# A decoder trunk on one core: other homes in SBUF for the operands of TensorE

## The chip, the core and the metric

The kernel runs on 1 core of one Trainium2 chip. The metric is the time of one execution in microseconds, as the device reports it; lower is better. A core has TensorE (PE; its weight loads are listed apart as PEld), VectorE (DVE), ScalarE (ACT), GpSimd (POOL) and SyncE (SP), which issues most of the DMAs. SBUF, the memory that the engines read their operands from, has 128 partitions; a tile has one home, a range of bytes, which is the same in each partition it spans.

## What is computed

Two layers of a decoder trunk on 256 tokens of width 1024, in float32. Each layer is a half-step SwiGLU with LayerNorm, three token mixers in parallel on one normalised stream, an output projection with LayerNorm, and a second half-step SwiGLU with LayerNorm.

```python
def hybrid_layer(x, mem_n, ...):
    h = layer_norm(ALPHA * x + 0.5 * swiglu(x, ffn1_w_gu, ffn1_w_down), ln_g[0], ln_b[0])
    (dn_q, dn_k, dn_v, dn_b, dn_a, dn_z, sw_q, sw_k, sw_v, xa_q, gates) = jnp.split(h @ w_in, split_idx, axis=-1)
    o_dn = deltanet_branch(...)            # gated delta rule, 4 heads of 128
    o_sw = sliding_window_attention(...)   # 8 query heads of 64, window 128, sinks
    o_xa = memory_cross_attention(...)     # 4 heads of 128 over 256 memory rows
    branches = jnp.stack([o_dn, o_sw, o_xa], axis=2)
    gates = sigmoid(gates.reshape(B, S, 3, D))
    merged = sum(gates * einsum('bsnc,ncd->bsnd', branches, w_branch), axis=2)
    h = layer_norm(ALPHA * h + merged @ w_out, ln_g[1], ln_b[1])
    return layer_norm(ALPHA * h + 0.5 * swiglu(h, ffn2_w_gu, ffn2_w_down), ln_g[2], ln_b[2])
```

`swiglu(x, w_gu, w_down)` is `(silu(gate) * up) @ w_down` with 2816 columns for each of gate and up.

## The kernel before

All weights come as one long stream from DRAM (`wst`), in units of 128 partitions x 1024 columns (512 KB), in the order of their use. `unit` (from line 99) loads a unit with a DMA on SP's queue into one of three buffers `raw` and splits it in two: ScalarE rounds it into `whi`, VectorE puts the remainder into `wlo` (`split`, line 116 in the profile's lists, five buffers of each). A product of full precision is then three matmuls in a fast format (`mm3`): high by high, high by low, low by high. The matmuls are recorded by one helper on line 125, those of the first block of an FFN also on lines 318, 319 and 321. The order of the instructions on an engine is that of a scheduler, with some stretches held in the order of the program.

A matmul has a stationary operand, which a weight load brings into TensorE, and a moving one, which is streamed past it. The names in the profile stand as `out<-moving,stationary`. Every matmul here is preceded by its own weight load. The kinds that matter:

- The transposed stream `hT` (eight blocks of 128 channels, high and low halves, 16 KB a partition) is stationary in the FFNs' first projections and in the gates; the split weights move, 512 columns at a time (`acc<-whi,hT`, `acc<-wlo,hT`). In the combined input projection of the mixers 324 columns move, and where an output is wanted transposed (`projB`) the split weights are stationary and 256 columns of `hT` move (`acc<-hT,whi`).
- The FFN's inner columns after the SwiGLU stand in `u0` to `u10`, each 4 KB a partition: 2 of the 22 column blocks, with high and low halves. They are stationary in the second projection (`acc<-whi,u`), block by block from `u0` on, 12 matmuls of 512 columns for most blocks. The mixers use `u0` to `u13` and `w0` to `w3` again for their own tiles, among them the branches' outputs, the memory's transposed rows and the merged stream (`w0` to `w3`).
- The last units of a second projection or of the output projection are split ahead of time into `u` and `w` tiles that are free by then and in `gt` and `pp`; there the names read `acc<-u,u` or `acc<-u,w`.

Tiles get their homes by pool, in the order in which the pools are opened, and within a pool by a tag's first use:

```python
pc = ctx.enter_context(tc.tile_pool(name="pc", bufs=1))
praw = ctx.enter_context(tc.tile_pool(name="praw", bufs=3))
phi = ctx.enter_context(tc.tile_pool(name="phi", bufs=5))
plo = ctx.enter_context(tc.tile_pool(name="plo", bufs=5))
pu = ctx.enter_context(tc.tile_pool(name="pu", bufs=1))
p2 = ctx.enter_context(tc.tile_pool(name="p2", bufs=2))
...
def T(pool, shape, tag, dt=F32, bufs=None):
    kw = {} if bufs is None else {"bufs": bufs}
    return pool.tile(shape, dt, tag=tag, name=nm(tag), **kw)
```

`pc` holds constants, masks, the residual stream `h0` and `h1` and the window attention's keys `swk`; `pu` holds `hT`, the `u` and `w` tiles and all that exists once; `p2` and `p3` hold what is used in turns (`t2`, `pt`, `pp`, `gt`). A slice of `hT`, of a `u` or `w` tile or of a split weight, as a matmul takes it, always starts at a multiple of 512 bytes from the tile's start, save for the 324 columns mentioned.

Of the kernel before, what the change touches and what calls it, by code (L numbers as in the profile page):

```python
# [37 lines left out]
@with_exitstack  # L38
def tile_trunk(ctx, tc, x, xT, mem, memT_, wst, lnp, memln, cvw, rows, cst, out):
    nc = tc.nc  # L40
    pc = ctx.enter_context(tc.tile_pool(name="pc", bufs=1))
    praw = ctx.enter_context(tc.tile_pool(name="praw", bufs=3))
    phi = ctx.enter_context(tc.tile_pool(name="phi", bufs=5))
    plo = ctx.enter_context(tc.tile_pool(name="plo", bufs=5))
    pu = ctx.enter_context(tc.tile_pool(name="pu", bufs=1))
# [8 lines left out]
    def nm(s):  # L54
        uid[0] += 1
        return f"{s}_{uid[0]}"

    def T(pool, shape, tag, dt=F32, bufs=None):
        kw = {} if bufs is None else {"bufs": bufs}
        return pool.tile(shape, dt, tag=tag, name=nm(tag), **kw)  # L60

    def acc():
        return T(psA, [P, 512], "acc")

    def at():
        return T(psT, [P, 512], "at")

    def sm():
        return T(psS, [P, 512], "sm")
# [161 lines left out]
    def new_hT():  # L231

        t = T(pu, [P, KD, 2, S], "hT", F32R)
        return t[:, :, 0, :], t[:, :, 1, :], t
# [791 lines left out]
    hT = new_hT()  # L1026
# [20 lines left out]
    for l in range(NL):  # L1047
# [18 lines left out]
        if not last:  # L1066
            f1, hT = Ffn(), post.hT
# [88 lines left out]
```

## Time and profile before

| | |
|---|---|
| time, median of 3 runs (lowest to highest) | 1295.89 us (1292.63 to 1296.61) |
| the profiled execution: its time, its span | 1294.92 us, 1293.1 us |
| granted TensorE clock, mean over the span | 0.995 |
| busy: PE, PEld, DVE, ACT, POOL | 1269.7, 1076.4, 855.6, 662.0, 201.2 us |
| DMA | 263.50 MB, mean 204 GB/s |

The span reaches from the first to the last instruction of the program. The duration of a matmul runs from its start to its end, and since matmuls are pipelined, the next one starts before that; the spacing of the starts is worked out from the first and last start of a group and its count. Rows of groups show count, busy time, mean duration and the idle time of the engine before them with what ended it; rows of a single tile show duration as min/median/max, and first and last start.

### The profile page before, as it was taken

The page shows a single profiled execution, that of the slowest core. Times are in us where ns is not written, and L with a number is a line of the kernel's source. Part 1 is how long each engine was busy: PE and PEld are TensorE (multiplying, and loading weights), DVE is VectorE, ACT ScalarE, POOL GpSimd, SP SyncE. Part 2 cuts the span into 40 slices and gives each one's busy share as a digit, 9 for nine tenths or more (in the row PEclk, how much of TensorE's full clock was granted, in tenths as well). Part 3 has the DMA queues.
Part 4 walks back from the last instruction along what each step waited for, and adds up shares of the span by engine and source line. Part 5 has one row for each costly group of instructions (what it writes and reads, how often), then busy time and mean ns, then how long its engine had stood idle before and what let it go on. Part 6 is the DMA issues. An engine that isn't in the chain of part 4 may idle for free.

```text
span 1293.1 us, 18743 instructions
## 1 busy us (share of the span) xinstructions
PE 1269.7 (98%) x6944; PEld 1076.4 (83%) x6944; DVE 855.6 (66%) x1273; ACT 662.0 (51%) x979; POOL 201.2 (16%) x361
## 2 busy tenths in 40 slices
PE   8999899999999999999999999999999999999997
PEld 6887688999878788888888888899988787888886
DVE  5676557698555776665676665758866378766555
ACT  5555443566574545454445444446556655455441
POOL 1232100102411002221012220000023100022200
PEclk9999899999999999999999999999999999999999
DMA  7887763654543648877768776656554256487762
GB/s 265 300 286 250 245 235 124 215 174 131 148 159 125 202 134 268 257 243 219 256 202 263 246 237 214 205 165 205 169 142 155 98 174 234 140 265 242 238 217 102
DMA packets 78075, 263.50 MB, mean 204 GB/s; under 512 B 11968, under 2 KB 13120, under 8 KB 77984
## 3 DMA queue, kind: packets, MB, share of 16 engines
q1 hardware_dynamic: 66320, 232.53, 54.8%
q0 software_dynamic: 11664, 29.77, 7.9%
q8 instruction: 54, 0.88, 0.3%
q14 instruction: 37, 0.30, 0.1%
HBM read 247.45 MB, written 14.81 MB: 203 GB/s over the span
## 4 chain that ended last, share of the span: by engine, by line
PE 83%; DMA 7%; DVE 4%; ACT 3%; issue 2%; POOL 0%; SPq 0%; DVEq 0%; ACTq 0%; POOLq 0%
PE acc L125 72%; DMA raw<-in_wst_dram 6%; PE at L125 4%; PE sm L125 3%; DVE wlo L116 2%; ACT whi L116 2%; PE sm L128 1%; PE acc L321 1%; PE acc L318 1%; PE acc L319 1%; PE at L128 1%; DVE u L116 0%; DMA gB<-ms 0%; DMA tr<-t 0%; ACT pp L724 0%
## 5 line engine op out<-in xcount | busy, mean ns | idle before, releaser
L116 DVE TENSOR_TENSOR wlo<-raw,whi 128x1024 fp32r<-128x1024 f32 (+2 forms) x403 | 484.8, 1209 | 331.9 <-ACT whi L116 329.5
L116 ACT CAST whi<-raw 128x1024 fp32r<-128x1024 f32 (+2 forms) x403 | 415.3, 1036 | 442.2 <-PE acc L125 209.8
L125 PE MATMUL acc<-whi,hT 128*128 128x512 f32 (+1 forms) x1824 | 563.6, 387 | 5.0 <-ACT whi L116 5.0
L125 PEld LDWEIGHTS acc<-whi,hT 128*128 128x128 f32 x1824 | 341.1, 188 | 73.1 <-ACT whi L116 5.0
L125 PE MATMUL acc<-wlo,hT 128*128 128x512 f32 (+1 forms) x912 | 351.1, 385 | 0.8 <-DVE wlo L116 0.8
L125 PE MATMUL acc<-whi,u 128*128 128x512 f32 x784 | 256.1, 400 | 5.9 <-DVE t L340 5.9
L125 PEld LDWEIGHTS acc<-wlo,hT 128*128 128x128 f32 x912 | 171.9, 188 | 34.5 <-DVE wlo L116 2.3
L125 PEld LDWEIGHTS acc<-whi,u 128*128 128x128 f32 x784 | 149.2, 190 | 42.2 <-DVE t L340 4.8
L125 PE MATMUL acc<-wlo,u 128*128 128x512 f32 x392 | 155.8, 398 | 0.0
L349 POOL DMA_DIRECT2D tr<-t x176 | 96.6, 556 | 354.6 <-DVE t L343 339.4
L125 PE MATMUL acc<-hT,whi 128*128 128x256 f32 x672 | 122.2, 284 | 0.0
L125 PEld LDWEIGHTS acc<-hT,whi 128*128 128x128 f32 x672 | 104.7, 192 | 0.0
L125 PE MATMUL acc<-hT,wlo 128*128 128x256 f32 x336 | 95.0, 283 | 0.0
L125 PEld LDWEIGHTS acc<-wlo,u 128*128 128x128 f32 x392 | 74.7, 191 | 16.5
L125 PEld LDWEIGHTS acc<-hT,wlo 128*128 128x128 f32 x336 | 64.4, 192 | 0.0
L350 POOL DMA_DIRECT2D pt<-tr x44 | 25.1, 571 | 183.5 <-DMA tr<-t 132.7
L339 ACT ACTIVATE t<-acc 128x256 f32<-128x256 f32 x88 | 32.9, 379 | 22.7 <-PE acc L125 22.7
L340 DVE TENSOR_TENSOR t<-t,acc 128x256 f32<-128x256 f32 x88 | 36.3, 417 | 6.5 <-ACT t L339 3.6
L116 DVE TENSOR_TENSOR u<-pt,u 128x512 fp32r<-128x512 f32 x44 | 29.0, 659 | 12.1 <-ACT u L116 12.1
L524 DVE SCALAR_TENSOR_TENSOR t<-acc,cw,t 128x255 f32<-128x255 f32 (+2 forms) x72 | 34.5, 479 | 0.9
L116 ACT CAST u<-pt 128x512 fp32r<-128x512 f32 x44 | 27.0, 613 | 14.4 <-DMA pt<-tr 14.4
L125 PE MATMUL acc<-whi,w 128*128 128x512 f32 x96 | 31.7, 401 | 2.1 <-DVE w L116 2.1
(248 smaller groups left out, 1188.5 us busy)
## 6 DMA issues: line engine op xcount, KB each, us to landing
raw<-in_wst_dram SPq DMA_DIRECT2D x409, 512.0 KB, 4.3
tr<-t POOLq DMA_DIRECT2D x176, 64.0 KB, 3.6
pt<-tr POOLq DMA_DIRECT2D x44, 256.0 KB, 4.7
raw<-in_wst_dram SPq DMA_DIRECT2D x16, 324.0 KB, 2.9
gB<-in_lnp_dram SPq DMA_DIRECT2D x6, 512.0 KB, 6.1
bB<-in_lnp_dram SPq DMA_DIRECT2D x6, 512.0 KB, 5.6
mdr<-w POOLq DMA_DIRECT2D x4, 512.0 KB, 7.2
w<-dr POOLq DMA_DIRECT2D x4, 512.0 KB, 10.6
```

The source lines that it names most:

```text
L116: return nc.scalar.copy(hi, src).ins, nc.vector.tensor_tensor(lo, src, hi.bitcast(F32), op=ALU.subtract).ins
L125: return pe(nc.tensor.matmul(*a, **k))
L128: return pe(nc.tensor.transpose(*a))
L318: nc.tensor.matmul(ps, hT[0][:, k, ts], hi[:, c], start=k == 0, stop=False)
L319: nc.tensor.matmul(ps, hT[0][:, k, ts], lo[:, c], start=False, stop=False)
L321: nc.tensor.matmul(ps, hT[1][:, k, ts], hi[:, c], start=False, stop=k == KD - 1)
L339: act = nc.scalar.activation(t[:, :, tb, :], g, AF.Silu).ins
L340: ins = nc.vector.tensor_tensor(t[:, :, tb, :], t[:, :, tb, :], u, op=ALU.mult).ins
L349: nc.gpsimd.dma_start(d[:, :, q].rearrange("b c x -> c b x"), z[32 * q:32 * q + 32].rearrange("c (b x) -> c b x", b=4))
L350: nc.gpsimd.dma_start(y, d.rearrange("b c q x -> (b c) (q x)"))
L524: nc.vector.scalar_tensor_tensor(yc[:, j, d:], b[:, j, :S - d], w[:, t:t + 1], yc[:, j, d:], op0=ALU.mult, op1=ALU.add)
```

## The change

A new pool `pn` is opened ahead of all others, and the tiles with the tags `hT`, `u0` to `u13` and `w0` to `w3`, which were in `pu`, are put there. All else keeps its pool, and pools behind it move up.

```diff
+    pn = ctx.enter_context(tc.tile_pool(name="pn", bufs=1))
     pc = ctx.enter_context(tc.tile_pool(name="pc", bufs=1))
     praw = ctx.enter_context(tc.tile_pool(name="praw", bufs=3))
     phi = ctx.enter_context(tc.tile_pool(name="phi", bufs=5))
...
+    NEAR = {"hT"} | {f"u{i}" for i in range(14)} | {f"w{i}" for i in range(4)}
+
     def T(pool, shape, tag, dt=F32, bufs=None):
+        pool = pn if pool is pu and tag in NEAR else pool
         kw = {} if bufs is None else {"bufs": bufs}
         return pool.tile(shape, dt, tag=tag, name=nm(tag), **kw)
```

The two built programs have the same instructions on each engine in the same order, with the same shapes and the same waits; the homes alone differ. Bytes within a partition, from the first to behind the last, and in brackets the first byte modulo 128:

| tiles | before | after |
|---|---|---|
| `hT` | 87584 to 103968 (32) | 16512 to 32896 (0) |
| `u0`, `u1`, `u2` | 103968 to 116256 (32) | 32896 to 45184 (0) |
| two small tiles, 320 bytes | 116256 to 116576 | 177696 to 178016 |
| `w0` to `w3` | 116576 to 132960 (96) | 45184 to 61568 (0) |
| `u3` to `u13`, with `gB` and `bB` among them before | 132960 to 186208 (96) | 61568 to 106624 (0), `gB` and `bB` at 178016 |
| constants, `swk` (`swk` at 32), `h0`, `h1` | 16512 to 34336 | 106624 to 124448 |
| `raw`, 3 buffers | 34336 to 46624 (32) | 124448 to 136736 (32) |
| `whi`, 5 buffers | 46624 to 67104 (32) | 136736 to 157216 (32) |
| `wlo`, 5 buffers | 67104 to 87584 (32) | 157216 to 177696 (32) |
| `sql` (the window attention's low queries) | 187840 to 191936 (64) | the same |
| `t2`, `pt`, `pp`, `gt` | 192992 to 225760 (96) | the same |

## The prediction

> **What bounds the kernel now.** I read the page first (engines, slices, the chain that ended last), then the waits of TensorE, then the groups kept apart by shape, then single tiles in short stretches.
>
> ```profile
> PE 1269.7 (98%) x6944; PEld 1076.4 (83%) x6944; DVE 855.6 (66%) x1273; ACT 662.0 (51%) x979; POOL 201.2 (16%) x361
> PEclk9999899999999999999999999999999999999999
> PE 83%; DMA 7%; DVE 4%; ACT 3%; issue 2%; POOL 0%; SPq 0%; DVEq 0%; ACTq 0%; POOLq 0%
> ...
> PE acc L125 <- DVE t L340: 5.9, 4, 3.4
> PE acc L125 <- ACT whi L116: 5.0, 1, 5.0
> PE acc L125 <- DVE w L116: 2.1, 2, 1.3
> ```
>
> TensorE is busy for 98% of the span at the full granted clock, it carries 83% of the chain, and its longest wait in total is 5.9 us. So the time is the number of matmuls times the spacing of their starts, and I look for what sets that spacing. The next rows are three stretches in which TensorE never waits: the first projection of an FFN with hT as the stationary operand, then the same second projection with u0 to u2 and, right behind it, with u3 to u7 as the stationary operand. Each shows count, duration (min/median/max) and first and last start.
>
> ```profile
> L125 PE MATMUL acc<-whi,hT x305: 389/389/389, 481.4 to 584.8; 128*128 128x512 f32 x153
> L125 PE MATMUL acc<-wlo,hT x153: 389/389/389, 481.6 to 585.0; 128*128 128x512 f32 x153
> ...
> L125 PE MATMUL acc<-whi,u x48: 388/389/389, 590.2 to 606.3; 128*128 128x512 f32 x48
> L125 PE MATMUL acc<-wlo,u x24: 389/389/389, 590.4 to 606.1; 128*128 128x512 f32 x24
> ...
> L125 PE MATMUL acc<-whi,u x80: 388/396/398, 606.3 to 633.8; 128*128 128x512 f32 x80
> L125 PE MATMUL acc<-wlo,u x40: 393/396/398, 606.7 to 634.0; 128*128 128x512 f32 x40
> ...
> L125 PE MATMUL acc<-hT,whi x14: 283/283/283, 243.2 to 245.5; 128*128 128x256 f32 x14
> L125 PE MATMUL acc<-hT,wlo x7: 283/283/283, 243.1 to 245.3; 128*128 128x256 f32 x7
> ...
> L125 PE MATMUL acc<-w,whi x29: 279/279/284, 203.1 to 208.0; 128*128 128x256 f32 x29
> L125 PE MATMUL acc<-w,wlo x15: 280/280/280, 203.2 to 208.2; 128*128 128x256 f32 x15
> ```
>
> Spacing from these: hT 103.6 us over 457 steps, 226.7 ns; u0 to u2 16.1 us over 71, 226.8 ns; u3 to u7 27.7 us over 119, 232.8, which the alternating durations of 393 and 398 put at 233.3 (duration less 162, as 389 goes with 226.7). The instruction, its shape, the clock and the moving buffers are the same; only the stationary tile differs. The 256-wide ones with hT moving and a split weight stationary run at 120 (2.4 us over 20 steps); with a w tile moving at some 117, since their durations are 279 and 280 for 283. From 226.7 and 120, 256 columns cost 106.7 ns, so 13.3 ns a matmul are left over beside the columns; with u3 and up that is 20, and in the w rows about 10.
>
> What differs is the address. The step lies between u2, which ends at byte 116,256 of the partition, and w0, which starts at 116,576: between them are two small tiles of 320 bytes. From there on every tile starts 64 bytes later in a block of 128. I call d the first byte of the moving operand less the first byte of the stationary one, modulo 128. hT and u0 to u2 have d = 0 (both operands at 32 of 128), u3 to u13 and w0 to w3 have d = -64 (moving at 32, stationary at 96), and in the w rows the moving operand is at 96 and the stationary at 32, d = +64. So left-over time against d reads: -64: 20 ns, 0: 13.3 ns, +64: some 10 ns, the last at the other width.
>
> **The change part by part.** No instruction is added, removed or moved on any engine or queue, and no wait changes; addresses do. hT, u and w go to 0 of 128, whi and wlo stay at 32. So d becomes +32 wherever a split weight moves past hT, u or w, and -32 where hT or w moves past a split weight. No row has these distances with TensorE in its steady state, so the price is bounded. The counts:
>
> ```profile
> L125 PE MATMUL acc<-whi,hT 128*128 128x512 f32 x1696 | 534.3, 392 | 5.0 <-ACT whi L116 5.0
> L125 PE MATMUL acc<-wlo,hT 128*128 128x512 f32 x848 | 331.2, 391 | 0.8 <-DVE wlo L116 0.8
> L125 PE MATMUL acc<-whi,u 128*128 128x512 f32 x784 | 256.1, 400 | 5.9 <-DVE t L340 5.9
> L125 PE MATMUL acc<-wlo,u 128*128 128x512 f32 x392 | 155.8, 398 | 0.0
> L125 PE MATMUL acc<-hT,whi 128*128 128x256 f32 x672 | 122.2, 284 | 0.0
> L125 PE MATMUL acc<-hT,wlo 128*128 128x256 f32 x336 | 95.0, 283 | 0.0
> L125 PE MATMUL acc<-whi,w 128*128 128x512 f32 x96 | 31.7, 401 | 2.1 <-DVE w L116 2.1
> L125 PE MATMUL acc<-u,w 128*128 128x512 f32 x108 | 26.1, 394 | 0.0
> L125 PE MATMUL acc<-w,whi 128*128 128x256 f32 x128 | 24.0, 283 | 0.0
> L318 PE MATMUL acc<-whi,hT 128*128 128x512 f32 x48 | 19.2, 401 | 0.0
> L125 PE MATMUL acc<-wlo,w 128*128 128x512 f32 x48 | 18.9, 394 | 0.0
> L125 PE MATMUL acc<-w,wlo 128*128 128x256 f32 x64 | 18.0, 282 | 0.0
> ```
>
> At d = +32 and 512 columns the low end is the slope of the table, 6.7 ns for 64 bytes: 3.3 ns below 226.7, 223.3. The high end is the slowest steady row, 233.3. Nearest in distance is the steady row at d = 0, and the table falls to the right of it, so I take the middle of 223.3 and 226.7: 225.0.
>
> - hT stationary: 1696 + 848, and 48 on each of the lines 318, 319 and 321, is 2688; 1.7 ns less each, -4.6 us (between -9.1 and +17.7).
> - u and w stationary under split weights: 784 + 392 + 96 + 48 = 1320. Of these u0 to u2 hold 6 of the 22 column blocks in each of 4 second projections, 12 matmuls a block: 288 at -1.7, -0.5 us (-1.0 to +1.9). The other 1032 go from 233.3 to 225.0: -8.6 us (-10.3 to 0).
> - Split weights stationary, 256 wide: 1008 with hT moving and 192 with w. The slope gives 123.3 for d = -32, the one row off d = 0 gives 117; middle 120.2. hT +0.2 us, w +0.6 us (together -3.0 to +4.5).
> - Last units of the second and output projections, which stand in u and w themselves: both operands move together, d stays 0, and 108 at 394 settle nearer 389: -0.5 us.
> - Work of the other engines on moved tiles: 0. ScalarE's and VectorE's splits already write into both regions at the same price, and they lie under the matmuls; if that cover were gone, 4 ns on 403 splits would be 2 us:
>
> ```profile
> L116 ACT CAST whi<-raw 128x1024 fp32r<-128x1024 f32 x385 | 402.3, 1051 | 423.1 <-DMA raw<-in_wst_dram 195.5 <-PE acc L125 193.4 <-issue 17.5
> L116 ACT CAST u<-raw 128x1024 fp32r<-128x1024 f32 x18 | 18.9, 1049 | 20.5 <-DMA raw<-in_wst_dram 20.0 <-DVE u L116 0.4
> ...
> 606.50:634.30 27.80, 27.80 (x121) 22.39 (x120) 15.94 (x14) 13.54 (x14) 0.00 (x0) 1.00 0.73 244
> ```
>
> - Supply: in that stretch VectorE works 15.9 of 27.8 us, ScalarE 13.5, and the DMA engines 0.73 at 244 GB/s. Matmuls 3.6% faster ask for 253 GB/s, and the same row's share would be 0.76; nothing else is late next.
>
> Sum: -4.6 - 0.5 - 8.6 + 0.8 - 0.5 = -13.4 us. The profiled execution took 1294.92 us (span 1293.1, 1.8 around it), 1.0 below the median of the runs shown; it becomes 1281.5. With 226.7 and 120 everywhere it would be -7.3, 1287.6; with the slope on both sides -9.1 - 1.0 - 10.3 + 4.5 - 0.5 = -16.4, 1278.5.
>
> The SBUF page of the Trainium skill (SBUF — State Buffer, "SBUF: two separate sides" and "Who interferes with whom") speaks against all of this: TensorE has one read port for the moving operand and another, independent one for loading weights, and it never waits for anyone. By that rule where tiles lie is worth nothing and the sum is 0. The trace does not agree in the stretches above, where 226.7 becomes 233.3 under otherwise equal conditions.
>
> **The rivals.** *A distance of +32 is a bad one (slower).* Only d = 0 is steadily quick at 512 columns. A tile at d = -32 (sql as stationary), and one at d = 0 whose moving operand lies 128 bytes further in a block of 256 (pp), show the next start 230 ns later:
>
> ```profile
> 353.57 0.63 PE L125 MATMUL at<-swk,u 128*128 128x512 f32 x2
> 354.04 0.40 PE L125 MATMUL at<-swk,sql 128*128 128x512 f32 x1
> 354.27 0.40 PE L125 MATMUL acc<-whi,hT 128*128 128x512 f32 x1
> ...
> 640.97 0.40 PE L125 MATMUL acc<-pp,u 128*128 128x512 f32 x1
> 641.20 0.39 PE L125 MATMUL acc<-u,u 128*128 128x512 f32 x1
> ```
>
> If every 512-wide matmul falls to 233.3, hT pays 17.7 us and u0 to u2 1.9, less 0.5: 1314. Halfway, at 230, it is +8.9 + 1.0 - 3.4 - 0.5 = +6.0, 1301. It decides from the mean that the 4008 matmuls have now, (2976 x 226.7 + 1032 x 233.3) / 4008 = 228.4: any steady spacing above that makes the kernel slower. Against it: towards negative d, 32 bytes cost the 3.3 ns of the slope (the 230 of sql) and 64 bytes twice that, and nothing but pp, a single matmul, shows a cost on another way.
>
> *It is the height in the partition, not the distance.* Stationary tiles low are quick, high ones slow; then 1032 matmuls gain 6.6 ns and nothing else moves: -6.8 - 0.5, 1287.6. For it: all slow tiles lie above 116,576. Against it: it needs a border exactly at the 320 bytes of two small tiles, and u2, which reaches 116,256, is still quick.
>
> *Nothing happens.* The spacing follows something else that u3 to u7 share, and the independent ports hold: 1294.9.
>
> **How the numbers follow.** About 0.3%, 3.9 us, is what a measurement of this kernel can tell from no change. My forecast has 0.45, height 0.12, nothing 0.12, the bad distance 0.31 (of which 0.08 only halfway). Faster: the first two less 0.02 for a small gain, 0.55; same 0.14; slower 0.31. The forecast's own range is 1275 to 1290. For 8 in 10 the range has to reach into the slow case: 1275 to 1311 leaves out most of the 0.23 at 1314 and above and a little below.
>
> **What would show it.** In the profile after, the long hT stretch should have durations near 387 and a spacing near 225; the second projection should show no step between u2 and u3; the 256-wide ones with hT should stay within 3 ns of 283. Durations of 393 or more in the hT stretch make the prediction wrong in its sign, 389 there with 389 for all u speaks for height, and a step that stays at u3 says that neither height nor distance was it. Splits that are longer on ScalarE or VectorE, or TensorE waiting for them, would show a cost that I set at 0.

## The result: 1.2% slower, and the profile after

The changed kernel takes 1310.96 us (median of 5 runs, 1308.86 to 1311.50) against 1294.43 us of the kernel before (median of 5): ratio 1.0121, 95% interval 1.0110 to 1.0132. The profiled execution took 1311.12 us, 16.2 more than the one before. The forecast was 1281.5; the sign is wrong, and the time lies at the very end of the range of 1275 to 1311, which had been stretched into the slow case. The time is near the 1314 of the rival "a distance of +32 is a bad one", although, as the runs below show, the distance is not +32.

From the profile after, the busy times, the granted clock and the chain that ended last; below them, from the same kernel, the list of TensorE's waits (total, times, longest):

```profile
PE 1289.6 (98%) x6944; PEld 1079.1 (82%) x6944; DVE 857.3 (65%) x1273; ACT 663.2 (51%) x979; POOL 199.9 (15%) x361
...
PEclk9999899999999999999999999999999999999999
...
PE 89%; DMA 3%; DVE 3%; ACT 3%; issue 1%; POOL 0%; DVEq 0%; ACTq 0%; POOLq 0%
```

```profile
PE acc L130 <- ACT whi L121: 4.9, 1, 4.9
PE acc L130 <- DVE t L345: 4.1, 2, 3.1
PE acc L130 <- DVE w L121: 0.9, 2, 0.5
PE sm L133 <- DVE h L287: 0.9, 2, 0.7
PE at L133 <- ACT pt L741: 0.8, 2, 0.4
```

TensorE is busy for 19.9 us more (1269.7 before), at the same clock, and its share of the chain rises from 83% to 89%. VectorE, ScalarE and GpSimd are busy as long as before within 2 us. TensorE's listed waits are even shorter: 11.6 us for 15.3.

The same stretches as in the prediction, with count, duration (min/median/max) and first and last start: the long run of hT, then the second projection, first its first 71 matmuls and then those up to its last units.

```profile
L130 PE MATMUL acc<-whi,hT x294: 392/397/400, 489.8 to 592.7; 128*128 128x512 f32 x147
L130 PE MATMUL acc<-wlo,hT x147: 392/397/400, 490.3 to 592.9; 128*128 128x512 f32 x147
...
L130 PE MATMUL acc<-whi,u x47: 392/397/400, 594.8 to 611.0; 128*128 128x512 f32 x47
L130 PE MATMUL acc<-wlo,u x24: 392/398/400, 595.0 to 611.2; 128*128 128x512 f32 x24
...
L130 PE MATMUL acc<-whi,u x81: 392/397/400, 611.4 to 639.5; 128*128 128x512 f32 x81
L130 PE MATMUL acc<-wlo,u x41: 392/397/400, 611.2 to 639.3; 128*128 128x512 f32 x41
```

The spacing of hT is 103.1 us over 440 steps, 234.3 ns (226.7 before). The step at u3 is gone, but both sides of it now stand where the slow side stood: 16.4 us over 70 steps, 234.3, and 28.3 over 121, 233.9. The 256-wide matmuls with hT last as long as before (284 and 283 ns); those with w, 283 before, are 3 ns longer:

```profile
L130 PE MATMUL acc<-hT,whi 128*128 128x256 f32 x672 | 122.3, 283 | 0.0
...
L130 PE MATMUL acc<-w,whi 128*128 128x256 f32 x128 | 24.4, 286 | 0.0
```

### The profile page after: what moved, and what is told of

Its sections match the earlier page's. It is cut to its first block, busy times and chain, and to the rows that moved or that the text cites. A ratio compares the mean times of both kernels' runs of the same rounds, so it can differ in the third digit from the quotient of the medians.

```text
span 1309.3 us, 18743 instructions
## 1 busy us (share of the span) xinstructions
PE 1289.6 (98%) x6944; PEld 1079.1 (82%) x6944; DVE 857.3 (65%) x1273; ACT 663.2 (51%) x979; POOL 199.9 (15%) x361
## 4 chain that ended last, share of the span: by engine, by line
PE 89%; DMA 3%; DVE 3%; ACT 3%; issue 1%; POOL 0%; DVEq 0%; ACTq 0%; POOLq 0%
PE acc L130 79%; PE at L130 3%; PE sm L130 3%; DMA raw<-in_wst_dram 2%; PE sm L133 1%; ACT whi L121 1%; PE acc L326 1%; PE acc L323 1%; PE acc L324 1%; DVE wlo L121 1%; PE at L133 1%; DMA gB<-ms 0%; DVE u L121 0%; DMA ms<-mst 0%; ACT pp L729 0%
## 5 line engine op out<-in xcount | busy, mean ns | idle before, releaser
L130 PE MATMUL acc<-whi,hT 128*128 128x512 f32 (+1 forms) x1824 | 576.0, 393 | 4.9 <-ACT whi L121 4.9
L130 PE MATMUL acc<-wlo,hT 128*128 128x512 f32 (+1 forms) x912 | 357.0, 391 | 0.0
L348 DVE STREAM_TRANSPOSE t<-t 128x512 f32<-128x512 f32 x44 | 31.3, 710 | 1.1
```

Of the source, the lines that this page charges most:

```text
L130: return pe(nc.tensor.matmul(*a, **k))
L348: ins = nc.vector.transpose(z, t.rearrange("p j t x -> p (j t x)")).ins
```

## The experiments

Eleven kernels ran, two of them with matmuls alone. The table puts the nine whole ones beside the two kernels compared. Distances are those of the two first bytes, moving less stationary, **modulo 256**, as the first map below showed that they have to be counted; many of the expectations still count modulo 128. The spacing of hT is that of the long run, from first and last start; that of the 256-wide ones is the mean over those which follow without a wait, without the few spaced by more than 150 ns.

| kernel | 512 wide: hT, u3 up | spacing of hT, ns | 256 wide with hT, ns | ratio to before [95%] |
|---|---|---|---|---|
| before | 0, 192 | 226.7 | 0: 119.9 | 1 |
| the change | 160, 160 | 234.3 | 96: 119.9 | 1.0121 [1.0110, 1.0132] |
| a_equal | 0, 0 | 226.7 | 0: 119.8 | 0.9963 [0.9951, 0.9976] |
| b_equal | 0, 0 | 226.7 | 0: 119.7 | 0.9977 [0.9965, 0.9989] |
| b_swap | 64, 0 | 228.8 | 192: 114.7 | 0.9963 [0.9948, 0.9977] |
| a_128 | 128, 128 | 232.4 | 128: 119.0 | 1.0074 [1.0052, 1.0096] |
| only_hT | 160, 192 | 234.3 | 96: 119.9 | 1.0097 [1.0076, 1.0118] |
| only_uw | 0, 160 | 226.6 | 0: 119.9 | 1.0013 [1.0003, 1.0024] |
| a_64 | 192, 192 | 233.3 | 64: 117.6 | 1.0080 [1.0066, 1.0094] |
| gap160 | 64, 64 | 228.8 | 192: 113.8 | 0.9976 [0.9967, 0.9986] |
| best | 0, 0 | 226.7 | 192: 116.4 | 0.9939 [0.9920, 0.9959] |

**map: the cost by itself.** A kernel of its own, with nothing but stretches of matmuls:

```python
for n in (512, 256, 324):
    for st in stat:                    # sa to sp, each 32 bytes further modulo 512
        run(st, mov, n)                # 72 matmuls; stationary blocks st[k], moving mov[0 or 1]
for off in (1, 2, 4, 6, 10, 12):       # elements of 4 bytes
    run(stat[0], mov, 512, off)
...                                    # then pairs with other tiles, 512 columns
```

> This kernel leaves the whole computation out: it copies x to the output and runs stretches of 72 fp32r matmuls by themselves, each with its own weight load, no other engine at work. The moving tile is held, 16 stationary tiles sa to sp begin 32 bytes further each in a block of 512 (so the moving start less the stationary start, mod 128, is 0, -32, -64, +32 four times over), at 512, 256 and 324 columns; then stationary starts 4 to 48 bytes further inside sa, a far pair at equal phase, and five pairs with another moving tile. Phase theory (only the distance of the two starts in a block of 128 counts): at 512 columns 226.7 ns for sa, se, si, sm and for far, 230 to 234 for the other twelve, the same after a move of both; at 256 columns 120 at equal phase and 117 to 120 elsewhere. Period longer than 128 (the pp row of the prediction): only sa at 226.7. Rival 'both on one side of the middle': all tiles lie below byte 95,000, so all at 226.7. Rival 'contention with the other engines' and transfers': with nothing else at work all stretches alike, at or below 226.7.

Its TensorE rows by time, 512 columns: sa is at distance 0, each further letter 32 bytes less, so sb 224, sc 192, sd 160, se 128, sf 96, sg 64, sh 32, si 0 again. Below them pairs of other tiles: sd moving past sb is 64, past sl 256, that is 0.

```profile
L52 PE MATMUL acc<-mov,sa x72: 389/389/397, 39.4 to 55.5; 128*128 128x512 f32 x72
L52 PE MATMUL acc<-mov,sb x72: 392/395/397, 55.7 to 72.3; 128*128 128x512 f32 x72
L52 PE MATMUL acc<-mov,sc x72: 393/396/398, 72.5 to 89.1; 128*128 128x512 f32 x72
L52 PE MATMUL acc<-mov,sd x72: 391/397/400, 89.3 to 105.9; 128*128 128x512 f32 x72
L52 PE MATMUL acc<-mov,se x72: 390/393/404, 106.2 to 122.7; 128*128 128x512 f32 x72
L52 PE MATMUL acc<-mov,sf x72: 392/394/399, 122.9 to 139.5; 128*128 128x512 f32 x72
L52 PE MATMUL acc<-mov,sg x72: 388/392/398, 139.7 to 156.0; 128*128 128x512 f32 x72
L52 PE MATMUL acc<-mov,sh x72: 389/395/397, 156.2 to 172.8; 128*128 128x512 f32 x72
L52 PE MATMUL acc<-mov,si x72: 389/389/397, 173.0 to 189.1; 128*128 128x512 f32 x72
...
L52 PE MATMUL acc<-sd,sb x72: 388/392/396, 747.6 to 763.9; 128*128 128x512 f32 x72
...
L52 PE MATMUL acc<-sd,sl x72: 388/389/393, 814.4 to 830.5; 128*128 128x512 f32 x72
```

Over the last 36 starts of each stretch: 0: 226.7 ns, 32: 233.3, 64: 228.9, 96: 233.3, 128: 232.4, 160: 234.3, 192: 233.3, 224: 233.3. The eight tiles si to sp repeat the first eight to 0.1 ns, and the pairs with sd agree to 0.2: at 512 columns only the distance counts, with a period of 256 (not of 128: se, at 128, is not quick). All tiles lie below byte 95,000 and no other engine works, so neither the height nor contention with other engines is needed; the durations of sd, 391 to 400, are those of the changed kernel. The 256-wide order is another one: 120.0 at 0 and 96, 118.7 at 128, 118.3 at 224, 117.8 at 32, 64 and 192, 117.4 at 160. So distance 0 is the best at 512 columns and one of the two worst at 256. At 324 columns the period does not hold throughout: sa and si, both at distance 0, have 146.7 and 149.3 ns, while the other seven pairs of tiles agree to 0.1; why is open.

**a_equal, b_equal, b_swap: whole kernels.** The first is the change with two gaps, the others are the kernel before with one. Each gap also gets a `memset` on GpSimd, left out here:

```diff
 # a_equal (the change)
+    gap = pc.tile([P, 24], F32, name="gap")
...
+    gap2 = p2.tile([P, 8], F32, name="gap2")
 # b_equal (the kernel before)
+        if tag == "w0" and not spacer:
+            spacer.append(pu.tile([P, 48], F32, name="gap"))
 # b_swap (the kernel before; in pu, ahead of hT)
+    gap = pu.tile([P, 48], F32, name="gap")
```

> The changed kernel with a gap of 96 bytes ahead of the constants and 64 ahead of t2: places stay (operands of the FFN low, split weights high), but moving and stationary tiles all start at 128 of 512. Phase theory: 512-wide spacing 226.7 for hT and all u; against before -6.8 us (1032 x 6.6), +0.5 for projB, -0.5 for the tails: 1287.6, ratio 0.995, and 23 us below the change. Rival 'both on one side of the middle of the partition' (before: hT, u0 to u2 and the split weights below 116,300, quick; u3 and up beyond it, slow; after: split weights beyond it, all slow): no change against after, 1311, ratio 1.012.

> The kernel before with a gap of 192 bytes ahead of w0: places stay, but w0 to w3 and u3 to u13 now start at 32 of 512 as hT, u0 to u2 and the split weights do. Phase theory: the step at u3 goes, 1032 matmuls gain 6.6 ns, -6.8 us, +0.5 for the 256-wide ones with w: 1288, ratio 0.995. Rival 'one side of the middle': nothing moves, 1294.4, ratio 1.000.

> The kernel before with the same gap of 192 bytes ahead of hT instead: hT and u0 to u2 now start at 96 of 128 (distance -64), w0 to w3 and u3 up at 32 (distance 0). Phase theory: the two kinds swap, hT and u0 to u2 233.3 (2976 x 6.6 = +19.6), u3 up 226.7 (-6.8), the 256-wide ones with hT 117.6 instead of 120 (-2.4), w the other way (+0.5): +10.9, 1305, ratio 1.008. Rival 'one side of the middle': no change, 1294.4.

In a_equal the long run of hT and the matmuls of u beyond u3 have one duration, although stationary tiles are low and split weights high:

```profile
L134 PE MATMUL acc<-whi,hT x295: 389/389/389, 488.0 to 588.0; 128*128 128x512 f32 x148
...
L134 PE MATMUL acc<-whi,u x81: 389/389/389, 605.0 to 632.2; 128*128 128x512 f32 x81
```

With 96 bytes ahead of the constants the loss of the change turns into a gain of 0.37%, and in b_equal the old homes with 192 bytes more give 0.23%. That settles "one side of the middle": both kernels have operands on either side of it. Neither gained all that was expected: a_equal 4.8 us of 6.8, b_equal 3.0 of 6.3. b_swap went against the expectation in sign: hT was slow by modulo 128 (-64), but it is at 64 modulo 256, 228.8 instead of 233.3, and the 256-wide ones gained 5.2 ns each, 5.2 us in all, where 2.4 had been expected (114.7 is a mean of two kinds, see best):

```profile
L127 PE MATMUL acc<-whi,hT x292: 388/390/392, 487.8 to 587.6; 128*128 128x512 f32 x146
```

**a_128: modulo 128 or 256.** A gap of 224 bytes in place of the 96.

> The changed kernel with a gap of 224 bytes ahead of the constants: distance 128 for the 512-wide ones. Distance counts modulo 256 (the map): spacing 232.4, 4008 x 5.6 = +22 us on a_equal by the sum, less some 4 that TensorE then waits less (the change itself had 15.3 us of waits before and 11.6 after), less 1 for the 256-wide ones: 1307 to 1312, ratio 1.010 to 1.013. Modulo 128, as the prediction had it: the same as a_equal, 1290.7, ratio 0.997.

```profile
L132 PE MATMUL acc<-whi,hT x289: 390/393/404, 487.6 to 588.0; 128*128 128x512 f32 x145
```

100.4 us over 432 steps, 232.4 ns, as the map has it at 128, with the map's odd duration of 404. Distance 0 modulo 128 does not make it quick. The time, 0.74% above before, lies some 3 us below the range expected.

**only_hT and only_uw: the change in two parts.** `NEAR = {"hT"}` in the one, the u and w tags alone in the other.

> One part of the change alone: only hT moves to the low end; u, w and split weights keep their distances. Distance theory: hT 160 mod 256, spacing 234.3, +19 us by the sum of 2688 x 7.1; u0 to u2 stay at 226.7, u3 up at 233.3; 256-wide ones 120. Less some 4 us of waits: 1309 to 1314, ratio 1.011 to 1.015, so the whole loss of the change. If the low homes of u and w carry part of the loss: under 1305.

> The other part of the change alone: u0 to u13 and w0 to w3 move to the low end, hT stays where it was. Distance theory, from the map: u0 to u2 160 mod 256 (+2.1 us for 288), u3 up from 192 to 160 (233.3 to 234.3, +1.0), 192 256-wide ones with w 117.6 to 119.9 (+0.4), tails -0.5; sum +3.0. In the runs so far about 0.7 of such a sum reached the time (only_hT 12.6 us of 19, a_128 14.4 of 20.5 against a_equal): +2.1, ratio 1.0016. If a low home by itself costs or gains something, it shows here as more than 1.004 or less than 0.999.

The long run of hT in only_hT:

```profile
L130 PE MATMUL acc<-whi,hT x294: 392/397/400, 489.7 to 592.5; 128*128 128x512 f32 x147
```

Most of the loss is that of hT: 0.97%, a little under what was expected; that of u and w is 0.13%. The two add up to 1.10% where the change has 1.21%.

**a_64 and gap160: a place in between.** Gaps of 32 and of 160 bytes ahead of the constants.

> The changed kernel with a gap of 32 bytes ahead of the constants: distance 64 for the 512-wide ones (map: 228.9) and 192 for the 256-wide ones (map 117.8; 116.4 in the kernel best). Against before: hT +4.7 us, u0 to u2 +0.5, u3 up -4.5, 256-wide -3.7, tails -0.7: -3.7, of which 0.7 reaches the time: -2.6, ratio 0.998. If distance 64 were as slow as its neighbours 32 and 96 (233.3): +11, ratio 1.009.

> The run a_64 was at distance 192, not 64 (split weights at 64, hT at 128 of 256; 64 less 128): its 233.3 ns is the map's value for 192. Here the gap is 160 bytes, split weights at 192, hT at 128, distance 64 in truth. By the map 228.9 for the 512-wide ones: sum against before -3.7 us, of which 0.7 reaches the time, -2.6, ratio 0.998. If only distance 0 were better than 232 in the whole kernel: 1.006 or more.

a_64 was built on a slip: I added 32 to the +32 of the prediction, but the split weights then begin at 64 and hT at 128 of 256, a distance of 192, so it tested that instead, and by the map's 233.3 it should be 1.009; 1.0080 was measured. gap160, put at 64 in truth, met its ratio of 0.998 with 0.9976, in part by luck: its 256-wide ones ran at 113.8 ns, where 116.4 to 117.8 had been reckoned with. The long runs of hT, first a_64, then gap160:

```profile
L132 PE MATMUL acc<-whi,hT x287: 393/394/399, 487.8 to 587.9; 128*128 128x512 f32 x144
```

```profile
L132 PE MATMUL acc<-whi,hT x287: 388/388/392, 488.0 to 586.2; 128*128 128x512 f32 x144
```

**map2: which pair, which order, which type.**

```python
run(pairs((mov, hi[2]), (lo[0], lo[2])), 512, 96)   # alternating; own distance 0, to the next load 192 or 64
run(pairs((mov, hi[2]), (lo[2], lo[0])), 512, 96)   # alternating; own 192 or 64, to the next 0
for i in range(8): run(proj(i), 256, 96)            # order of the input projections
for i in range(8): run(plain(bst[i], bmov), 512, 96)  # bf16
```

> Again only matmuls by themselves, the computation left out. (1) Two stretches in which moving and stationary tiles alternate between two starts 64 bytes apart. In the first a matmul's own two operands are at distance 0 and its moving operand to the stationary one loaded next at 64 or 192 mod 256; in the second its own are at 64 or 192, and to the next at 0. Theory 'the moving read meets the load of the next stationary operand': first 231 ns (mean of the map's 233.3 and 228.9), second 226.7. Theory 'a matmul's own pair counts': the other way round. (2) 256 columns in the order of the input projections (high, high, low stationary tile; the low half of the moving operand 1024 bytes behind the high one), at eight distances: 120 at distance 0; 113 to 115 at 192 if the kernel b_swap's 114.7 is due to this order, 117.8 (as the first map had at 192) if not. (3) The same at 512 columns with bf16 operands, half the bytes: if the distance of byte addresses counts as in fp32r, 7 ns of spread over the eight; if it is the rate of bytes that makes it, one value for all.

Of the alternating stretches every second matmul, of the first and then of the second; below them bf16:

```profile
L53 PE MATMUL acc<-sc,tc x48: 388/393/396, 41.4 to 63.2; 128*128 128x512 f32 x48
L53 PE MATMUL acc<-sc,ta x48: 389/393/395, 63.7 to 85.4; 128*128 128x512 f32 x48
...
L53 PE MATMUL acc<-bmov,ba x94: 379/379/390, 176.8 to 197.3; 128*128 128x512 bf16 x94
L53 PE MATMUL acc<-bmov,bb x94: 379/379/380, 197.5 to 218.0; 128*128 128x512 bf16 x94
...
L53 PE MATMUL acc<-bmov,bd x94: 379/379/380, 238.9 to 259.4; 128*128 128x512 bf16 x94
```

In bf16 all eight distances have one duration, 379 ns, and one spacing, 215.8 (20.5 us over 95 steps; 2 of the 96 records of each stretch are missing from the trace). The question of the pair stays open: both alternating stretches settle at the same 231.7 ns (over their last 36 steps), so neither a matmul's own pair nor its pair with the next load decides alone. The order of the input projections is not what gave 114.7 either: here 192 has 117.8.

**best: homes by width.** Pools in the order pn, phi, plo, pc, praw; `whi` and `wlo` 64 columns wider; the 256-wide projections' units 16 columns further in, the others at the start. From its edit:

```diff
-    def unit(w=U, dst=None, cuts=1, behind=None):
+    def unit(w=U, dst=None, cuts=1, behind=None, at_=0):
...
-            hi = T(ph, [P, U], th, F32R)
-            lo = T(pl, [P, U], tl, F32R)
+            hi, lo = (T(q, [P, U if dst else U + 64], t, F32R)[:, at_:] for q, t in ((ph, th), (pl, tl)))
...
-            hi, lo = unit(behind=behind)
+            hi, lo = unit(behind=behind, at_=16)
```

To make room, `zero` became a column of `epsc`.

> Homes chosen by width: operands of the FFN low as in the change, split weights right behind them so that 512-wide ones are at distance 0 mod 256, and the units of the 256-wide projections (whi, wlo widened by 64 columns) put 64 bytes further into their tiles, distance 192. Distance theory: 512-wide as in a_equal (227.1), the 1008 256-wide ones with hT 114.7 instead of 119.8 (-5.1 us), 192 with w the same (-1.0): 1290.7 - 6.1 = 1284.6, up to 2 us of it given back as waits, ratio 0.992 to 0.994. If 114.7 was another effect: 1290.7, ratio 0.997.

1287.06 us, ratio 0.9939: 0.6% better than before and 1.8% better than the change. Its 256-wide ones come in two kinds, though. A stretch in which they run at the quick one:

```profile
L129 PE MATMUL acc<-hT,whi x61: 276/276/276, 239.8 to 250.0; 128*128 128x256 f32 x61
L129 PE MATMUL acc<-hT,wlo x30: 276/276/276, 240.0 to 249.9; 128*128 128x256 f32 x30
```

That is 10.2 us over 90 steps, 113.3 ns, and so does the like stretch of the second layer; the rest stay near 117.8, the map's value for the same distance.

## Why the prediction was wrong, step by step

**The mechanism held.** Only addresses differed; the spacing of TensorE's starts set most of the time; it follows the distance of the two operands; the step at u3 was an effect of it; and the height is no matter. Why the distance counts, and which read meets which, stays open. By the rule of the Trainium skill (SBUF — State Buffer, "Who interferes with whom": two independent read ports for the moving operand and for weight loads) nothing should have moved. The map, with nothing but TensorE at work, does not agree: 226.7 to 234.3 ns.

**The step that failed is the 225.0 ns at "d = +32".** The runs show 234.3 ns in its place, at a distance of 160 modulo 256. It failed in two ways.

- *The modulus.* Two distances in the kernel before, 0 and -64, had been long rows, and 128 was the smallest period that fitted them. hT stands at 128 modulo 256 after the change and the split weights at 32: the distance is -96, that is 160, and not +32. The one row which spoke against 128 was quoted as a rival's evidence and then set aside as a single matmul: pp, at distance 0 modulo 128 and 128 modulo 256, was not quick. Nor is it a single one: the trace of before has six such matmuls, each of 395 ns and with the next start 234 ns later. a_128 and the map show that the row was right (232.4).
- *The slope.* The line through -64, 0 and +64 took its right end from 256-wide rows. At 256 columns distance 0 is a slow one (120.0) and 64 a quick one (117.8); at 512 it is the other way (226.7 and 228.9). There is no slope: 32 would have been 233.3, so the forecast would have failed with the right distance as well.

The terms, with mean spacings before and after over the matmuls that follow without a wait. The few spaced far above the rest (over 290 ns, 256 wide over 150) are left out here and come below:

| term | predicted, us | spacing before, after, ns | by these, us |
|---|---|---|---|
| hT stationary, 2688 | -4.6 | 227.2, 234.2 | +18.8 |
| u0 to u2, 288 | -0.5 | 226.9, 234.3 | +2.1 |
| u3 up and w, 1032 | -8.6 | 233.3, 234.1 | +0.8 |
| 256 wide with hT, 1008 | +0.2 | 119.9, 119.9 | 0 |
| 256 wide with w, 192 | +0.6 | 117.6, 120.1 | +0.5 |
| last units in u and w, 192 | -0.5 | 230.2, 228.2 | -0.4 |
| splits, supply | 0 | | none seen |

The hT term lies 1.1 us above the upper end of its own range, 17.7, that of u0 to u2 0.2 above its 1.9, and the u3 term 0.8 above its upper end of 0. The last units came as forecast. The 256-wide ones did too, but by luck: the forecast's 120.2 was the middle between two guesses for a distance of -32, which is 224 modulo 256 and has 118.3 in the map, while the distance after is 96, which has 120.0. The forecast's figure of 1287.6 for "226.7 and 120 everywhere" leaves out the 0.6 us that the w rows lose then; it should be 1288.2. The splits came as forecast: ScalarE takes 1050 ns for one (1051 before), VectorE 1231 (1228 before):

```profile
L116 DVE TENSOR_TENSOR wlo<-raw,whi 128x1024 fp32r<-128x1024 f32 x385 | 470.3, 1228 | 312.2 <-ACT whi L116 309.8
...
L121 DVE TENSOR_TENSOR wlo<-raw,whi 128x1024 fp32r<-128x1024 f32 x385 | 472.0, 1231 | 329.2 <-ACT whi L121 328.1
L121 ACT CAST whi<-raw 128x1024 fp32r<-128x1024 f32 x385 | 402.5, 1050 | 440.2 <-PE acc L130 244.8 <-DMA raw<-in_wst_dram 148.1 <-issue 19.9
```

**The sum is +21.8, the time +16.2.** The rest was absorbed. The clearest place is the first layer, where TensorE idles as the second projection begins. Its rows up to 190 us, and the window from 120 to 140 us (span, PE busy, PEld, DVE, ACT, POOL, granted clock, DMA share, GB/s), of before and then of after:

```profile
L125 PE MATMUL acc<-whi,u x144: 388/393/793, 130.4 to 189.4; 128*128 128x512 f32 x144
...
120.00:140.00 20.00, 13.87 (x51) 9.59 (x49) 13.10 (x15) 11.25 (x18) 5.83 (x12) 0.90 0.83 300
```

```profile
L130 PE MATMUL acc<-whi,u x144: 390/397/795, 131.8 to 189.3; 128*128 128x512 f32 x144
...
120.00:140.00 20.00, 16.42 (x67) 12.36 (x65) 12.21 (x14) 11.04 (x17) 5.51 (x11) 0.94 0.84 282
```

The last of these matmuls starts at the same time in both. The slower first projection took away 2.5 us of idle time there (6.1 us of the 20 before, 3.6 after), and the granted clock in this window was 0.94 for 0.90. Over the whole kernel the listed waits shrank by 3.7 us. Another 1.8 us come from matmuls with u stationary that follow without a wait and yet start more than 290 ns apart: 41 before cost 5.8 us more than at the mean spacing, 29 after 4.0, and all but 0.1 of the 1.8 lies between 100 and 200 us. In the other direction the same took its share: a_equal's spacings are worth -6.7 us by the same sum, and its ratio gives -4.8, with 20.0 us of listed waits. I had costed the supply at nothing because no load was late in the steady stretch; the first layer was not that stretch. What TensorE waits for there stands in the trace of before (start, duration, and in brackets the idle time ahead and what ended it):

```profile
137.55 1.04 ACT L116 CAST whi<-raw 128x1024 fp32r<-128x1024 f32 x1 [3.09 <-DMA raw<-in_wst_dram]
138.62 1.23 DVE L116 TENSOR_TENSOR wlo<-raw,whi 128x1024 fp32r<-128x1024 f32 x1 [2.86 <-ACT whi L116]
139.77 0.41 DVE L340 TENSOR_TENSOR t<-t,acc 128x256 f32<-128x256 f32 x1
140.24 0.79 PE L125 MATMUL acc<-whi,u 128*128 128x512 f32 x1 [3.44 <-DVE t L340]
```

TensorE waits for VectorE's product `t` of the SwiGLU, VectorE stands ahead of it in a split that waits for ScalarE, and ScalarE waits for a weight load. So it is the supply; no run took this wait away.

## What to carry to other kernels

Where TensorE bounds a kernel with fp32r operands (the fast 4-byte format here) and a weight load for each matmul, read the spacing of matmul starts in a long stretch without waits, compare it with the other tiles of the same shape, and write down where both operands start modulo 256; here 32 bytes of padding decide about 3% of that spacing. Measure the cost by itself for every width before choosing homes: a map of 834 us answered what three values in the trace could not, and the best distance at 512 columns was one of the two worst at 256. And do not fit a period with two values: here one row that contradicted it weighed more than the two which agreed.

## What the runs showed of the hardware that was not expected

- The spacing of 512-wide fp32r matmuls has a period of 256 bytes in the distance of their operands, and it is not smooth: it depends on the distance down to 4 bytes. Stationary operands 4, 8, 16 and 24 bytes further in than distance 0 gave 232.3, 230.6, 233.3 and 230.0 ns. The six such stretches together:

```profile
L52 PE MATMUL acc<-mov,sa x432: 388/394/399, 614.6 to 714.7; 128*128 128x512 f32 x144
```

- bf16 operands show none of it, 215.8 ns at all eight distances. The Trainium skill (TensorE: Matmul & The Clock Gate, "Back-to-back issue gap") gives N / 2.4 + 2.5 ns for an isolated gap, by which an estimate for 512 columns is 215.8: the bf16 rows agree with that, the fp32r rows lie 11 to 19 ns above it. For a stream of matmuls with weight loads, which these are, the same section of the Trainium skill has some 131 ns; no 512-wide stretch here came below 215.8.
- One distance can hold more than one steady state. At a distance of 192 the same kind of 256-wide matmul settles at 113.3 ns (duration 276) or at 117.8 (281), and stays there to the end of the stretch; gap160 was in the first in most of its stretches, b_swap in about half, best in two long ones, both maps in the second throughout. What chooses is not known.
